# FFN gate and up projections: sixteen tile products per output tile replaced by seven block products

## The chip, the cores and the metric

The kernel runs on one core of a Trainium2 chip. The metric is device time in microseconds (us) for one execution. The engines are named as in the profile: PE (TensorE matmul) and PEld (its weight load), DVE (VectorE), ACT (ScalarE), POOL (GpSimd), and SP, which issues the DMAs.

## What is computed

A decoder trunk of two layers, 512 tokens, model width 1024, FFN width 2816, all in float32. Each layer is an attention mixer and then a SwiGLU FFN, both behind an adaptive norm:

```python
mod = cond @ ada_w[l] + ada_b[l]
sh1, sc1, g1, sh2, sc2, g2 = [m[:, None, :] for m in jnp.split(mod, 6, axis=-1)]
h = _rms_norm(x, norm_mix[l]) * (1.0 + sc1) + sh1
...
x = x + g1 * (y @ w_out[l])
h = _rms_norm(x, norm_ffn[l]) * (1.0 + sc2) + sh2
x = x + g2 * _swiglu(h, ffn_gate[l], ffn_up[l], ffn_down[l])

def _swiglu(h, wg, wu, wd):
    return (jax.nn.silu(h @ wg) * (h @ wu)) @ wd
```

## The kernel before

**Splitting.** Every operand of the large products is held as a pair: `hi`, the value rounded to the PE's fast float32 format (`FR`), and `lo`, what the rounding left. A product is three matmuls, hi with hi, hi with lo and lo with hi, added in PSUM (`mm3`, L437 to L438; the matmul itself is L431, in `mms`). A weight arrives by DMA as a `raw` tile of 128 x 2048 (1 MB) and is split in pieces of 512 columns: ACT copies a piece to `whi` (L457), DVE subtracts to get `wlo` (L473). For some early weights, in the attention, the subtraction of the upper two pieces is on POOL (`prep_to`). Three `raw`, three `whi` and three `wlo` buffers of 2048 columns are there.

**The FFN.** The work is feature-major: an output tile has 128 hidden features on the partitions and the tokens along the columns. There are 22 tiles (`FT`) per layer, in two parts of 11 (`FPARTS`). One unit of weights `wg` holds the gate and up weights of one tile: 8 contraction tiles of 128 for gate, then 8 for up. `ffn_tile` multiplies them with the normalised input `H` (8 tiles, hi and lo):

```python
ps = [self.ps("gu") for _ in range(2)]
for k in range(KT):
    for s in range(2):
        self.mm3(ps[s][:, c], hi[:, s, k], lo[:, s, k], H[k][0][:, c], H[k][1][:, c], k == 0, k == KT - 1)
sg = self.t2("sg")[:, c]
self.act(sg, ps[0][:, c], AF.Silu, after=self.lnexp)
self.tt(sg, ps[1][:, c], sg, OP.mult)
```

and then splits the result into `hid` (ACT copy, DVE subtraction). The first two tiles of a layer are done in token halves of 256 (`HALVES`), since the norm of the second half is not ready when the first is; the other 20 take all 512 tokens at once. After each part, `reduce_out` multiplies the 11 `hid` tiles with the down weights (`wd`) for 8 output tiles and adds them to `x` (L488, `x<-ps,mod,x`).

**Background.** In layer 0's FFN seven modulation vectors of `mod_rest` are computed on DVE beside the rest: each is 16 products of a 128 x 512 piece of `raw<-in_ada` with a column of `cond` (L481 for the first, L488 `t<-raw,cond,t` for those that add), about four such operations for each FFN tile.

**Order.** The builder records operations on virtual tiles; `Sched` puts them in one order with estimated durations (`ve_ns` and others), buffer limits (the groups of `Kern.__init__`) and, for DVE, due times worked out from when PE would want each result. The order of each engine is then fixed in the program. Every engine runs its own list strictly in that order.

Of the kernel before, what the change touches and what calls it, by code (L numbers as in the profile page):

```python
# [20 lines left out]
KT = 8  # L21
# [4 lines left out]
BIG = 1e30  # L26
TOPK = 128
# [50 lines left out]
class View:  # L78
# [32 lines left out]
    def region(self):  # L111
        """bits of the (32-partition quadrant, column block) pairs touched, and elements per partition"""
# [46 lines left out]
class Sched:  # L159
    CROSS, SAME, DMA = 270, 130, 2300  # L160
    # the PE's clock is halved at first and for a while after a long gap
# [54 lines left out]
    def due(self):  # L216
        """priorities from when the PE, kept busy in the present order, would want each result"""
# [151 lines left out]
class Kern:  # L369
    def __init__(self, ctx, tc, io, out):  # L370
        self.ctx, self.tc, self.nc, self.io, self.out = ctx, tc, tc.nc, io, out
        pool = lambda n, b, **k: ctx.enter_context(tc.tile_pool(name=n, bufs=b, **k))
        self.const = pool("const", 1)
        self.s = s = Sched(tc)
        s.group("raw", pool("raw", 3), 3, 0, None)
        s.group("whi", pool("whi", 3), 3, 0, None)
        s.group("wlo", pool("wlo", 3), 3, 0, None)
        n = 61
        s.group("t2", pool("t2", n), n, 8, None, L=12, pT=4, qf=3, q=8, nt=10, hid=26, ada0=20)
        s.group("sm", pool("sm", 80), 80, 16, None)  # L380
        s.group("ps", pool("ps", 8, space=PSUM), 8, 1, None, mm=3, lg=2, tp=2, pv=2, gu=4, st=7)
        self.bg = []

# [38 lines left out]
    def mms(self, jobs, dur=None):  # L422
        """matmuls issued one after the other: (out, stationary, moving, start, stop)"""
# [204 lines left out]
    def mod_first(self, k):  # L628
        """shift and scale of the first norm for the features of k-tile k"""
# [17 lines left out]
    def mod_rest(self, l, v, on_pe):  # L647
        """one of the six modulation vectors"""
        ps = acc = None
        for h in range(4):  # L650
# [3 lines left out]
            for e in range(2):  # L654
# [46 lines left out]
    def norm_stats(self, c, sums=None):  # L701
        """reciprocal root mean square of the tokens c, on every partition"""
# [28 lines left out]
    def proj_f(self, H, i, w, ncol, tag="mm"):  # L731
        """[128 tokens of block i, ncol]; w(k) -> hi, lo of k-tile"""
# [7 lines left out]
    def rstd(self, ss, nh, inv):  # L740
        """[P, nh] of sums of squares -> (ss * inv + eps) ** -0.5"""
# [24 lines left out]
    def q_t(self, ps, qs):  # L766
        """queries of one token block: norm, scale, transpose -> hi, lo [P (two heads), 4, 128 tokens]"""
# [18 lines left out]
    def y_out(self, ps, Y, i, gain=None):  # L786
        """psum [P, 4, 128] -> hi, lo of four k-tiles, tokens of block i"""
# [50 lines left out]
    def idx_scores(self, i, iq):  # L838
# [3 lines left out]
        # Dp is 1e30 where masked, below 512 elsewhere  # L842
# [44 lines left out]
    def pv_t(self, pv, T, src, V):  # L887
        """transposed outputs of eight heads: four on each half of the partitions"""
# [12 lines left out]
    def attn_c(self, i, hg, q, Y):  # L901
        """eight heads of one query block; keys of this block and the one before"""
# [355 lines left out]
```

## Time and profile before

| what | value |
|---|---|
| median of 3 runs | 1208.24 us (1208.17 to 1209.27) |
| profiled execution: span from the first to the last instruction | 1205.3 us |
| median above the span | 2.9 us |
| mean granted TensorE clock | 1.000 |
| PE busy | 1180.9 us, 98% of the span |
| DVE busy | 707.4 us, 59% |
| ACT busy | 487.1 us, 40% |
| POOL busy | 87.9 us, 7% |
| DMA | 151.58 MB, mean 126 GB/s |

The page gives the profiled execution by its span alone, so 2.9 us is what lies around it against the median. Busy time of PE counts matmuls that overlap in the pipeline; how fast matmuls really follow each other is read from the starts in the timeline. The same holds for DVE and ACT: an instruction's duration is somewhat longer than the distance to the next when several stand in a row.

### The profile page before, as it was taken

Reading aid. Unit: us, or ns where it says so; the run is one execution under the profiler, and the core shown is the slowest. Engines: PE = TensorE matmul, PEld = TensorE weight load, DVE = VectorE, ACT = ScalarE, POOL = GpSimd, SP = SyncE. Lnnn points to the kernel's source line nnn. Section 1 sums busy time; section 2 is a strip of 40 time slices with the busy share of each in tenths; the row PEclk is TensorE's granted clock in tenths of the full one; section 3 lists DMA queues with packets and bytes.
Section 4 is the critical chain, followed back from the end, with each engine's and each line's share of the span. In section 5 each row is a group of like instructions: output and inputs, shape, how many; then the busy total and the mean of one; then the engine's idle time right before and its main releaser. Section 6 shows DMA issues by size and latency. Waiting matters only on the chain.

```text
span 1205.3 us, 16639 instructions
## 1 busy us (share of the span) xinstructions
PE 1180.9 (98%) x6424; PEld 956.2 (79%) x6424; DVE 707.4 (59%) x1656; ACT 487.1 (40%) x1194; POOL 87.9 (7%) x224
## 2 busy tenths in 40 slices
PE   6989999999999999999999999999999999999998
PEld 3867667679988888888889876669988888888888
DVE  5599999847875456655443967748633323233321
ACT  5464376755433221232232666755423312223310
POOL 0142332300000000000000120100000000000000
PEclk9999999999999999999999999999999999999999
DMA  9545612202585546655511322011422223322211
GB/s 349 228 140 175 245 41 101 76 31 71 179 299 185 175 155 216 226 189 175 175 59 65 105 71 71 1 71 70 141 105 77 98 88 105 105 105 95 80 53 36
DMA packets 32415, 151.58 MB, mean 126 GB/s; under 512 B 3152, under 2 KB 4304, under 8 KB 21072
## 3 DMA queue, kind: packets, MB, share of 16 engines
q1 hardware_dynamic: 32336, 150.52, 35.6%
q8 instruction: 50, 0.82, 0.3%
q14 instruction: 29, 0.24, 0.1%
HBM read 148.41 MB, written 2.10 MB: 125 GB/s over the span
## 4 chain that ended last, share of the span: by engine, by line
PE 89%; DVE 7%; ACT 2%; issue 1%; POOL 0%; DMA 0%; SPq 0%; DVEq 0%; POOLq 0%; ACTq 0%
PE ps L431 86%; PE ps L442 3%; DVE t L488 2%; ACT t L457 1%; DVE wlo L473 1%; DVE sm L857 1%; DVE t L858 1%; DVE t L473 1%; DVE t L493 1%; DVE t L481 1%; DMA x<-in_x 0%; POOL sm L473 0%; DVE sm L499 0%; ACT whi L457 0%; ACT sm L457 0%
## 5 line engine op out<-in xcount | busy, mean ns | idle before, releaser
L431 PE MATMUL ps<-t,whi 128*128 128x512 f32 (+2 forms) x2864 | 774.7, 358 | 0.9 <-ACT t L457 0.9
L431 PEld LDWEIGHTS ps<-t,whi 128*128 128x128 f32 x2864 | 506.7, 189 | 82.8 <-issue 4.5
L431 PE MATMUL ps<-t,wlo 128*128 128x512 f32 (+2 forms) x1432 | 509.9, 356 | 0.0
L431 PEld LDWEIGHTS ps<-t,wlo 128*128 128x128 f32 x1432 | 270.6, 189 | 38.1
L457 ACT ACTIVATE t<-ps 128x512 f32<-128x512 f32 (+6 forms) x274 | 120.3, 475 | 399.5 <-PE ps L431 372.2
L457 ACT ACTIVATE whi<-raw 128x512 fp32r<-128x512 f32 x364 | 206.8, 621 | 163.3 <-PE ps L431 98.9
L473 DVE TENSOR_TENSOR wlo<-raw,whi 128x512 fp32r<-128x512 f32 x340 | 221.8, 691 | 38.7 <-ACT whi L457 38.3
L473 DVE TENSOR_TENSOR t<-ps,t 128x128 fp32r<-128x128 f32 (+4 forms) x120 | 56.2, 489 | 220.5 <-PE ps L431 202.1
L431 PE MATMUL ps<-whi,t 128*128 128x512 f32 (+1 forms) x512 | 172.9, 394 | 1.1 <-DVE t L488 1.1
L431 PEld LDWEIGHTS ps<-whi,t 128*128 128x128 f32 x512 | 95.0, 189 | 29.5 <-issue 7.8
L488 DVE SCALAR_TENSOR_TENSOR x<-ps,mod,x 128x512 f32<-128x512 f32 (+1 forms) x64 | 39.3, 616 | 115.2 <-PE ps L431 114.7
L431 PE MATMUL ps<-wlo,t 128*128 128x512 f32 (+1 forms) x256 | 96.5, 377 | 0.0
L488 DVE SCALAR_TENSOR_TENSOR t<-raw,cond,t 128x512 f32<-128x512 f32 x112 | 79.1, 761 | 19.5 <-DMA raw<-in_ada 19.5
L431 PE MATMUL ps<-t,t 64*128 64x256 f32 (+5 forms) x592 | 82.8, 347 | 0.2 <-ACT t L457 0.2
L431 PEld LDWEIGHTS ps<-t,t 64*128 64x128 f32 (+2 forms) x592 | 54.3, 181 | 28.4 <-issue 15.1
L457 ACT ACTIVATE t<-t,sm 128x256 f32<-128x256 f32 (+3 forms) x128 | 65.5, 516 | 20.4 <-DVE sm L493 12.6
L442 PE MATMUL ps<-cst,t 128*128 128x128 f32 x388 | 61.8, 279 | 10.0 <-DVE t L473 6.8
L442 PEld LDWEIGHTS ps<-cst,t 128*128 128x128 f32 x388 | 45.0, 140 | 32.6 <-issue 9.9
L481 POOL TENSOR_SCALAR sm<-sm 128x8 f32<-128x8 f32 (+2 forms) x64 | 18.4, 288 | 550.8 <-DVE sm L499 547.4
L473 DVE TENSOR_TENSOR t<-t,t 128x512 fp32r<-128x512 f32 (+3 forms) x85 | 50.2, 593 | 14.1 <-ACT t L457 13.9
L431 PEld LDWEIGHTS ps<-wlo,t 128*128 128x128 f32 x256 | 48.4, 189 | 6.2
L493 DVE CUSTOM_DVE_ANT_0 t<-ps,cst 128x256 f32<-128x256 f32 (+3 forms) x104 | 39.1, 409 | 18.5 <-PE ps L431 18.1
(72 smaller groups left out, 564.6 us busy)
## 6 DMA issues: line engine op xcount, KB each, us to landing
raw<-in_wg SPq DMA_DIRECT2D x44, 1024.0 KB, 4.8
raw<-in_ada SPq DMA_DIRECT2D x40, 1024.0 KB, 5.3
raw<-in_wd SPq DMA_DIRECT2D x20, 1024.0 KB, 4.7
raw<-in_w0c SPq DMA_DIRECT2D x10, 1024.0 KB, 6.1
t<-in_ada SPq DMA_DIRECT2D x32, 256.0 KB, 6.5
raw<-in_wo SPq DMA_DIRECT2D x8, 1024.0 KB, 4.8
raw<-in_w1c SPq DMA_DIRECT2D x6, 1024.0 KB, 4.7
x<-in_x SPq DMA_DIRECT2D x8, 256.0 KB, 5.1
```

The source lines that it names most:

```text
L431: self.nc.tensor.matmul(o.ap(), l.ap(), r.ap(), start=st, stop=sp, skip_group_check=True)
L442: self.s.op("PE", 107, lambda: self.nc.tensor.transpose(out.ap(), src.ap(), self.ident.ap()), [out], [src, self.ident])
L457: self.nc.scalar.activation(out.ap(), src.ap(), func, **kw)
L473: lambda: self.eng(e).tensor_tensor(out.ap(), a.ap(), b.ap(), op=op), [out], [a, b])
L481: self.eng(e).tensor_scalar(out.ap(), a.ap(), val(s1), val(s2), op0=op0, **kw)
L488: lambda: self.nc.vector.scalar_tensor_tensor(out.ap(), a.ap(), val(s), b.ap(), op0=op0, op1=op1),
L493: lambda: self.nc.vector.tensor_tensor_reduce(out.ap(), a.ap(), b.ap(), op0=OP.add, op1=OP.min, scale=scale, scalar=3e38, accum_out=accum. ...
L857: self.s.op("DVE", 65 + 1.05 * n, lambda m8=m8: self.nc.vector.max(m8.ap(), sc.ap()), [m8], [sc])
L858: self.s.op("DVE", 65 + 1.05 * n, lambda m8=m8: self.nc.vector.match_replace(sc.ap(), m8.ap(), sc.ap(), -3e38), [sc], [m8, sc])
```

## The change

For 20 of the 22 FFN tiles of each layer (all but the first two, `DIRECT`), the product of the pair gate and up with the input is written as a 2 x 2 block product: the contraction is cut into halves of 512, the outputs are gate and up, the tokens are cut into halves of 256. Of the eight block products a scheme of Strassen's kind makes seven. It needs sums of weight blocks (four per tile, on POOL, `prep_to`), sums of input blocks (once per layer, `combos`: additions on DVE, four subtractions of 256 columns per contraction tile on POOL, split on ACT and DVE), and sums of the products on the way to gate and up (`ffn_seven`). Each of the seven weight blocks of 512 columns is split into hi and lo as before.

The weight buffers become 26 single tiles of 512 columns (group `w`, in place of 3 + 3 of 2048), the general group goes from 61 to 59 tiles, and gate and up may take six PSUM banks in place of four. The estimate of a POOL operation goes from 2.1 to 2.48 ns per column. The rest of the diff is the same work with the new buffers (`chunk`, `reduce_out`, `ffn_tile`, `even`) and removed comments.

```diff
+NW, NT2 = 26, 59
+DIRECT = 2
...
-        s.group("whi", pool("whi", 3), 3, 0, None)
-        s.group("wlo", pool("wlo", 3), 3, 0, None)
-        n = 61
-        s.group("t2", pool("t2", n), n, 8, None, L=12, pT=4, qf=3, q=8, nt=10, hid=26, ada0=20)
+        s.group("w", pool("w", NW), NW, 6, None)
+        n = NT2
+        s.group("t2", pool("t2", n), n, 8, None, L=12, pT=4, qf=3, q=8, nt=10, hid=26, ada0=20, S=8, T=8)
...
-        s.group("ps", pool("ps", 8, space=PSUM), 8, 1, None, mm=3, lg=2, tp=2, pv=2, gu=4, st=7)
+        s.group("ps", pool("ps", 8, space=PSUM), 8, 1, None, mm=3, lg=2, tp=2, pv=2, gu=6, st=7)
...
         if e == "POOL":
-            return 165 + 2.1 * n
+            return 165 + 2.48 * n
...
-            for a in range(0, w, 512):
-                b = min(a + 512, w)
-                self.copy(hi[:, a:b], raw[:, a:b])
-                self.tt(lo[:, a:b], raw[:, a:b], hi[:, a:b].bitcast(F), OP.subtract, e="POOL" if a >= 1024 and 2 < i < 15 else "DVE")
-            self.ws[i] = (hi, lo)
+            step = 400 if name == "w0s" else 512
+            if name[:2] == "wg" and idx >= DIRECT:
+                X1, X2, Y1, Y2 = (raw[:, a:a + 512] for a in range(0, 2048, 512))
+                S = [self.s.tile("w", "S") for _ in range(4)]
+                for t, x, y, op in ((S[0], Y1, Y2, OP.add), (S[1], S[0], X1, OP.subtract),
+                                    (S[2], X1, Y1, OP.subtract), (S[3], X2, S[1], OP.subtract)):
+                    self.tt(t, x, y, op, e="POOL")
+                src = [X1, S[1], S[0], X2, S[2], S[3], Y2]
+            else:
+                src = [raw[:, a:min(a + step, w)] for a in range(0, w, step)]
+            self.ws[i] = []
+            for j, a in enumerate(src):
+                hi, lo = (self.s.tile("w", "w", dt=FR)[:, :min(step, w - j * step) if len(src) < 7 else 512] for _ in range(2))
+                self.copy(hi, a)
+                self.tt(lo, a, hi.bitcast(F), OP.subtract, e="POOL" if j >= 2 and 2 < i < 15 else "DVE")
+                self.ws[i].append((hi, lo))
...
+    def combos(self, H):
+
+        c1, c2 = HALVES
+        T = []
+        for k in range(4):
+            f = []
+            for j in (k, k + 4):
+                t = self.t2("T")
+                self.tt(t, H[j][0].bitcast(F), H[j][1].bitcast(F), OP.add)
+                f.append(t)
+            p, q = self.t2("T"), self.t2("T")
+            self.tt(p[:, c1], f[0][:, c2], f[0][:, c1], OP.subtract, e="POOL")
+            self.tt(p[:, c2], f[1][:, c2], p[:, c1], OP.subtract, e="POOL")
+            self.tt(q[:, c1], f[1][:, c2], f[0][:, c2], OP.subtract, e="POOL")
+            self.tt(q[:, c2], f[1][:, c1], p[:, c2], OP.subtract, e="POOL")
+            o = []
+            for t in (p, q):
+                hi, lo = self.t2("h", dt=FR), self.t2("h", dt=FR)
+                self.copy(hi, t)
+                self.tt(lo, t, hi.bitcast(F), OP.subtract)
+                o += [(hi[:, c], lo[:, c]) for c in HALVES]
+            T.append(o)
+        return T
+
+    def ffn_seven(self, H, T, w, hid):
+
+        c1, c2 = HALVES
+        a, b, e = (self.ps("gu")[:, c1] for _ in range(3))
+        B11 = [tuple(t[:, c1] for t in H[k]) for k in range(4)]
+        B21 = [tuple(t[:, c1] for t in H[k]) for k in range(4, 8)]
+        B22 = [tuple(t[:, c2] for t in H[k]) for k in range(4, 8)]
+        T1, T2, T3, T4 = ([T[k][j] for k in range(4)] for j in range(4))
+
+        def product(out, j, B, start=False):
+            for k in range(4):
+                wh, wl = (t[:, k * P:(k + 1) * P] for t in w[j])
+                self.mm3(out, wh, wl, B[k][0], B[k][1], start and k == 0, k == 3)
+        pq, u, sg = (self.t2("sg") for _ in range(3))
+        product(a, 0, B11, True)
+        self.copy(pq[:, c1], a)
+        product(b, 1, T2, True)
+        self.tt(b, b, pq[:, c1], OP.add)
+        self.copy(u[:, c1], b)
+        product(e, 2, T1, True)
+        self.copy(pq[:, c2], e)
+        product(a, 3, B21)
+        self.act(sg[:, c1], a, AF.Silu, after=self.lnexp)
+        product(b, 4, T3)
+        self.tt(u[:, c2], b, pq[:, c2], OP.add)
+        product(e, 5, B22)
+        self.tt(sg[:, c2], e, u[:, c1], OP.add)
+        self.act(sg[:, c2], sg[:, c2], AF.Silu)
+        product(b, 6, T4)
+        self.tt(sg[:, c1], b, sg[:, c1], OP.mult)
+        self.tt(sg[:, c2], u[:, c2], sg[:, c2], OP.mult)
+        self.copy(hid[0], sg)
+        self.tt(hid[1], sg, hid[0].bitcast(F), OP.subtract)
+        return sg
...
-                sg = self.ffn_tile(H, f, c, w(f), hid[f - a])
+                if f < DIRECT:
+                    sg = self.ffn_tile(H, f, c, w(f), hid[f - a])
+                else:
+                    T = T or self.combos(H)
+                    sg = self.ffn_seven(H, T, w(f), hid[f - a])
```

What the scheduler makes of it is seen in the engines' own lists. First DVE in the second part of layer 1's FFN, in the middle of the gate and up tiles, before the change (`wlo<-raw,whi` are the weight subtractions; `t<-ps,t` is the product of gate and up, the line with two `t` inputs the subtraction for `hid`):

```order
L473 TENSOR_TENSOR wlo<-raw,whi 128x512 x2
L473 TENSOR_TENSOR t_9999<-ps,t_9999 128x512
L473 TENSOR_TENSOR wlo<-raw,whi 128x512 x2
L473 TENSOR_TENSOR t_10025<-t_9999,t_10018 128x512
L473 TENSOR_TENSOR wlo<-raw,whi 128x512 x2
```

A tile has six DVE instructions of 512 columns there: four weight subtractions, the product and the subtraction. With the change, one tile at the same place (`w<-w` are subtractions on weight sums that POOL made):

```order
L474 TENSOR_TENSOR w<-raw,w 128x512
L474 TENSOR_TENSOR w<-w 128x512 x2
L474 TENSOR_TENSOR ps<-ps,t_13151 128x256
L474 TENSOR_TENSOR w<-raw,w 128x512
L474 TENSOR_TENSOR t_13191<-t_13075,t_13141 128x512
L474 TENSOR_TENSOR w<-w 128x512 x2
L474 TENSOR_TENSOR w<-raw,w 128x512
L474 TENSOR_TENSOR t_13186<-ps,t_13151 128x256
L474 TENSOR_TENSOR t_13217<-ps,t_13186 128x256
L474 TENSOR_TENSOR t_13217<-t_13186,t_13217 128x256
L474 TENSOR_TENSOR t_13217<-ps,t_13217 128x256
```

A tile has thirteen: seven weight subtractions, the `hid` subtraction, and five of 256 columns, one of which puts a sum back into PSUM (`ps<-ps,t`). Nine of the thirteen read two inputs in SBUF, four read PSUM and SBUF.

Then POOL at the start of layer 0's FFN, with the change. Before, POOL has nothing in the FFN: its last instruction on weights is a pair of `wlo<-raw,whi` for `w_out`.

```order
L474 TENSOR_TENSOR w<-raw 128x512
L474 TENSOR_TENSOR w<-w,raw 128x512
L474 TENSOR_TENSOR w<-raw 128x512
L474 TENSOR_TENSOR w<-raw,w 128x512
L474 TENSOR_TENSOR t_3985<-t_3971 128x256
L474 TENSOR_TENSOR t_3985<-t_3995,t_3985 128x256
L474 TENSOR_TENSOR t_4021<-t_3995,t_3971 128x256
```

The four weight sums of the first block-product tile stand ahead of the sixteen input sums of 256 columns, and the four weight sums of the next tile stand among these.

## Rows read from the trace of the kernel before

**Rows 1.** The page: busy time by engine, and the chain's shares.
```profile
PE 1180.9 (98%) x6424; PEld 956.2 (79%) x6424; DVE 707.4 (59%) x1656; ACT 487.1 (40%) x1194; POOL 87.9 (7%) x224
...
PE 89%; DVE 7%; ACT 2%; issue 1%; POOL 0%; DMA 0%; SPq 0%; DVEq 0%; POOLq 0%; ACTq 0%
```

**Rows 2.** Chain in order of time, its last piece: start us, us, what.
```profile
804.87 397.11 PE ps L431 x2048
```

**Rows 3.** Windows, four stretches: us, busy us (count) by engine, clock, DMA.
```profile
312.35:429.07 116.72, 116.72 (x566) 96.22 (x564) 75.03 (x126) 36.92 (x71) 0.00 (x0) 1.00 0.63 218
486.77:613.04 126.27, 126.27 (x574) 102.72 (x574) 64.75 (x106) 38.05 (x70) 0.00 (x0) 1.00 0.50 173
854.54:968.37 113.83, 113.83 (x536) 95.70 (x535) 41.73 (x73) 35.11 (x68) 0.00 (x0) 1.00 0.31 107
1021.48:1147.89 126.41, 126.41 (x559) 104.72 (x558) 43.07 (x71) 36.61 (x69) 0.00 (x0) 1.00 0.29 99
```

**Rows 4.** Timeline of PE in `w_out`, layer 0: start us, us, instruction, count.
```profile
275.85 0.62 PE L431 MATMUL ps<-t,whi 128*128 128x512 f32 x2
...
276.53 0.40 PE L431 MATMUL ps<-t,whi 128*128 128x256 f32 x2
...
287.32 0.40 PE L431 MATMUL ps<-t,whi 128*128 128x256 f32 x2
```

**Rows 5.** Timeline of DVE, FFN of layer 0, instructions in a row.
```profile
477.72 2.50 DVE L473 TENSOR_TENSOR wlo<-raw,whi 128x512 fp32r<-128x512 f32 x4 [1.73 <-ACT whi L457]
480.14 2.73 DVE L488 SCALAR_TENSOR_TENSOR t<-raw,cond,t 128x512 f32<-128x512 f32 x4
...
318.77 1.08 DVE L473 TENSOR_TENSOR t<-ps,t 128x256 f32<-128x256 f32 x3
```

**Rows 6.** Lines by form: count, busy us, mean ns of one, idle before.
```profile
L473 DVE TENSOR_TENSOR wlo<-raw,whi 128x512 fp32r<-128x512 f32 x339 | 221.5, 692 | 38.7 <-ACT whi L457 38.3
L473 POOL TENSOR_TENSOR wlo<-raw,whi 128x512 fp32r<-128x512 f32 x24 | 34.1, 1435 | 77.4 <-ACT whi L457 77.3
L488 DVE SCALAR_TENSOR_TENSOR t<-raw,cond,t 128x512 f32<-128x512 f32 x112 | 79.1, 761 | 19.5 <-DMA raw<-in_ada 19.5
L473 DVE TENSOR_TENSOR t<-ps,t 128x256 f32<-128x256 f32 x8 | 3.1, 418 | 3.9 <-ACT t L457 3.9
L473 POOL TENSOR_TENSOR sm<-sm 128x8 f32<-128x8 f32 x60 | 16.0, 267 | 23.2 <-ACT sm L457 20.2
```

**Rows 7.** Timeline of POOL and DVE, attention of layer 0, 63 to 70 us.
```profile
63.70 1.29 POOL L473 TENSOR_TENSOR wlo<-raw,whi 128x512 fp32r<-128x512 f32 x1 [0.38 <-ACT whi L457]
63.75 0.48 DVE L473 TENSOR_TENSOR t<-ps,t 128x128 fp32r<-128x128 f32 x2
64.15 1.39 DVE L473 TENSOR_TENSOR wlo<-raw,whi 128x512 fp32r<-128x512 f32 x1
...
66.90 1.63 DVE L473 TENSOR_TENSOR wlo<-raw,whi 128x512 fp32r<-128x512 f32 x1
67.95 1.74 POOL L473 TENSOR_TENSOR wlo<-raw,whi 128x512 fp32r<-128x512 f32 x1
68.46 1.78 DVE L473 TENSOR_TENSOR wlo<-raw,whi 128x512 fp32r<-128x512 f32 x1
```

**Rows 8.** The same two engines, attention of layer 0, at 100 and 174 us.
```profile
100.66 2.55 POOL L473 TENSOR_TENSOR wlo<-raw,whi 128x512 fp32r<-128x512 f32 x2 [3.86 <-ACT whi L457]
...
101.45 1.15 DVE L857 MAX8 sm<-t 128x8 f32<-128x512 f32 x2
...
174.54 1.54 POOL L473 TENSOR_TENSOR wlo<-raw,whi 128x512 fp32r<-128x512 f32 x1 [0.58 <-ACT whi L457]
...
174.19 2.44 DVE L488 SCALAR_TENSOR_TENSOR t<-raw,cond,t 128x512 f32<-128x512 f32 x2
...
177.38 1.46 DVE L488 SCALAR_TENSOR_TENSOR t<-raw,cond,t 128x512 f32<-128x512 f32 x1
```

**Rows 9.** Timeline of ACT, start of layer 1's FFN: the last half-tile silu.
```profile
862.58 0.38 ACT L457 ACTIVATE t<-ps 128x256 f32<-128x256 f32 x1 [2.02 <-PE ps L431]
```

More of the change, by code (lines that the diff above doesn't have):

```diff
@@ L482, in ts, with stt @@
         self.s.op(e, self.ve_ns(e, out.region()[1], a.base.group != "ps", len(ptr)), fn, [out], [a] + ptr)
-    def stt(self, out, a, s, b, op0, op1):
+    def stt(self, out, a, s, b, op0, op1, e="DVE"):
         ptr = [s] if isinstance(s, View) else []
         val = lambda v: v.ap() if isinstance(v, View) else v
-        self.s.op("DVE", self.ve_ns("DVE", out.region()[1], False, len(ptr)),
-                  lambda: self.nc.vector.scalar_tensor_tensor(out.ap(), a.ap(), val(s), b.ap(), op0=op0, op1=op1),
+        self.s.op(e, self.ve_ns(e, out.region()[1], False, len(ptr)),
+                  lambda: self.eng(e).scalar_tensor_tensor(out.ap(), a.ap(), val(s), b.ap(), op0=op0, op1=op1),
                   [out], [a, b] + ptr)
@@ L550, in prep_to @@
             w = self.units[i][2]
+            name, idx, _ = self.units[i]
             raw = self.raws.pop(i)
-            hi = self.s.tile("whi", "whi", (P, 2048), FR)
-            lo = self.s.tile("wlo", "wlo", (P, 2048), FR)
-            for a in range(0, w, 512):
-                b = min(a + 512, w)
-                self.copy(hi[:, a:b], raw[:, a:b])
-                self.tt(lo[:, a:b], raw[:, a:b], hi[:, a:b].bitcast(F), OP.subtract, e="POOL" if a >= 1024 and 2 < i < 15 else "DVE")
-            self.ws[i] = (hi, lo)
+            step = 400 if name == "w0s" else 512
[14 more added lines that the diff above has]
+                self.ws[i].append((hi, lo))
             self.prepped += 1
@@ L568, in chunk @@
     def chunk(self):
-        ua, ub = self.unit(), self.unit(2)
-        a, b = ([t.rearrange("p (k c) -> p k c", k=4) for t in u] for u in (ua, ub))
-        return lambda k: (a[0][:, k], a[1][:, k]) if k < 4 else (b[0][:, k - 4], b[1][:, k - 4])
+        ts = self.unit() + self.unit(2)
+        return lambda k: ts[k]
     def setup(self):
@@ L645, in mod_first, with mod_rest @@
         self.stt(self.G[0][0][:, k:k + 1], self.mod[0][:, 1, k:k + 1], 1.0, self.ng[:, 0, 0, k:k + 1], OP.add, OP.mult)
-    def mod_rest(self, l, v, on_pe):
+    def mod_rest(self, l, v, on_pe, e_="DVE"):
         ps = acc = None
@@ L951, in even @@
         self.score, self.iw, self.bv = {}, {}, {}
-        hi, lo = self.unit()
-        hi, lo = (t[:, :1600].rearrange("p (k c) -> p k c", k=8) for t in (hi, lo))
-        small = [self.proj_f(H, i, lambda k: (hi[:, k], lo[:, k]), 200, "st") for i in range(NB)]
+        ws = self.unit()
+        w0s = lambda k: tuple(t[:, (k % 2) * 200:(k % 2) * 200 + 200] for t in ws[k // 2])
+        small = [self.proj_f(H, i, w0s, 200, "st") for i in range(NB)]
         w = self.chunk()
@@ L1077, in block @@
             while len(blocks) <= j:
-                hi, lo = self.unit()
+                u = self.unit()
                 w = self.units[self.cursor - 1][2]
-                blocks.extend((hi[:, a:a + P], lo[:, a:a + P]) for a in range(0, w, P))
+                blocks.extend(tuple(t[:, a % 512:a % 512 + P] for t in u[a // 512]) for a in range(0, w, P))
             return blocks[j]
@@ L1104, in ffn_tile @@
             for s in range(2):
-                self.mm3(ps[s][:, c], hi[:, s, k], lo[:, s, k], H[k][0][:, c], H[k][1][:, c], k == 0, k == KT - 1)
+                wh, wl = (t[:, (k % 4) * P:(k % 4) * P + P] for t in w[2 * s + k // 4])
+                self.mm3(ps[s][:, c], wh, wl, H[k][0][:, c], H[k][1][:, c], k == 0, k == KT - 1)
         sg = self.t2("sg")[:, c]
@@ L1113, in ffn @@
     def ffn(self, l, H, last):
+        T = None
         for pi, (a, b) in enumerate(FPARTS):
@@ L1119, in w @@
                 if f not in W:
-                    W[f] = [t.rearrange("p (s k c) -> p s k c", s=2, k=8) for t in self.unit()]
+                    W[f] = self.unit()
                 return W[f]
@@ L1123, in ffn @@
             if pi == 0:
-                jobs = [(a + e, c) for c in HALVES for e in range(2)]
+                jobs = [(a + e, c) for c in HALVES for e in range(DIRECT)]
             jobs += [(f, ALL) for f in range(a + len(jobs) // 2, b)]
             for f, c in jobs:
-                sg = self.ffn_tile(H, f, c, w(f), hid[f - a])
+                if f < DIRECT:
[3 more added lines that the diff above has]
+                    sg = self.ffn_seven(H, T, w(f), hid[f - a])
                 self.lnexp = []
```

5 lines of the change are left out of this document (2 added, 3 removed).

## The prediction

> **What bounds the kernel now.** I read the page first: PE is busy for 98% of the span and holds 89% of the chain that ended last [rows 1]. The chain's last piece is 397.11 us of matmuls without a break, all of layer 1's FFN [rows 2]. So there only PE's own work counts, or whatever makes PE wait anew. The change touches four stretches, which the windows show [rows 3]: from the end of the norm to the first update of `x` (layer 0: A0, 116.7 us; layer 1: A1, 113.8 us), and from the last update of part 1 to the first of part 2 (B0, 126.3 us; B1, 126.4 us). PE is busy through all four, POOL does nothing, DVE works 75.0, 64.8, 41.7 and 43.1 us. Everything else, some 720 us, I take as unchanged: the same work with other buffers. Its order moves in places; the chain has 9% on DVE and ACT [rows 1], about 108 us, and a twentieth of that, 5 us either way, goes into the range (a choice).
>
> **PE: what the change takes away.** Matmuls of 512 columns start 0.68 us apart in threes (275.85 to 276.53), so 0.227 us each; of 256 columns 30 threes take 10.79 us (276.53 to 287.32), so 0.120 us each [rows 4]. A tile had 2 x 8 x 3 = 48 of the first kind, 10.88 us. It gets 7 x 4 x 3 = 84 of the second, 10.07 us. The eighth of the products that goes is mostly eaten by the dearer short matmul: 0.8 us is left per tile. That is 7.2 us in A0 and A1 (nine tiles), 8.8 us in B0 and B1 (eleven), 32 us in all.
>
> The Trainium skill (TensorE: Matmul & The Clock Gate, section Back-to-back issue gap) gives columns / 2.4 + 2.5 ns for matmuls in a row, so 216 and 109 ns; by that a tile would save 1.2 us, and the 40 tiles 15 us more than by the rows. The rows are of this kernel with its weight loads and decide.
>
> **DVE: what it adds.** In a row, 512-column subtractions come every 0.603 us ((2.50 - 0.69) / 3), background steps every 0.657 us ((2.73 - 0.76) / 3), 256-column operations every 0.33 us ((1.08 - 0.42) / 2) [rows 5, 6]. A tile had 6 x 0.603 = 3.6 us and gets 8 x 0.603 + 5 x 0.33 = 6.5 us. The input sums add 16 x 0.603 = 9.6 us per layer. On the windows of [rows 3] this gives A0 75.0 + 9 x 2.9 + 9.6 = 111, B0 97, A1 77, B1 75 us. Counting the changed DVE list between the same marks gives 105, 95, 76 and 74 (in A0 a few background steps now stand outside); I use these. All fit under PE's time. ACT gains three copies and some halves, about 3 us per tile; with 35 to 38 us in stretches of 114 to 126 us [rows 3] it stays below PE. No DMA is added, and SP issues in the same order.
>
> **POOL and DVE together.** POOL gets four 512-column operations per tile, some 1.3 us each when alone [rows 7], 5.2 us per tile of 10: it is not the bound itself. But it stood idle in the FFN, and the trace shows what it does to DVE. At 64 us DVE subtractions that read two SBUF inputs take 1.39, 1.63 and 1.78 us beside POOL's [rows 7], against 0.69 alone [rows 6]; POOL's fourth takes 1.74 us in place of 1.29. They take turns: DVE's end at 68.53 and 70.24, a period of 1.71 us for one of each. At 174 us two background steps take 2.44 us beside one POOL operation, against 0.76 + 0.657 in a row; one takes 1.46 [rows 8]. DVE operations that read PSUM, or one input, are not held up (0.48 us for two at 63.75, `MAX8` at 101.45) [rows 7, 8].
>
> So I charge DVE a wait d for each POOL operation of 512 columns. The hits cost 0.70, 0.94, 1.09, 1.03 and 0.70 us, mean 0.89. Bounds: 0, as beside `MAX8`, and 1.09. In the changed list 9 of 13 operations per tile read two SBUF inputs, and in layer 0 the background steps come on top, so nearly each POOL operation should hit: I take 0.89. POOL's 16 input sums of 256 columns cost (1435 + 267) / 2 = 0.85 us each [rows 6] and hold DVE about half as long. A0 has 32 + 8, the other stretches 40 such units (those of the first tile come earlier): 40 x 0.89 = 36 us more for DVE.
>
> The Trainium skill (SBUF — State Buffer, section Who interferes with whom) says that with two SBUF inputs on DVE against a reading GpSimd instruction the second to start fully blocks until the first is done. Taken at its word, every POOL operation would cost DVE its whole length, which is the third rival below; by the rows, where a pair overlaps by about 0.2 us and some waits are partial, it is less.
>
> **The start of each FFN.** The input sums need the whole norm. In layer 1 it ends at 854.5 [rows 3] and the half tiles at about 862.6 [rows 9]. POOL then has 16 x 0.85 + 4 x 1.3 = 19 us in a row, plus about 2 us for the split behind it: T complete at about 875 to 880. PE has, without T, two products of each of two tiles, 48 x 0.12 = 5.8 us, and half of T's products, 2.9 us: until 871. I take 8 us of waiting per layer (0 to 12).
>
> **The shared PSUM bank.** In `ffn_seven` the product that ends in `b` needs DVE's reading of `b` one product earlier: 12 matmuls, 1.44 us of cover. One subtraction in the way and the 0.42 us reading take 1.11 us, but 2.2 us when POOL is in the way (1.78 + 0.42) [rows 6, 7]. That is 0 to 0.8 us per tile; I take 0.4 for the 20 tiles of layer 1, 8 us. In layer 0 DVE's time counts it already.
>
> **The sum.** A0: DVE 105 + 36 = 141 against 116.7, +24. B0: 95 + 36 = 131 against 126.3, +5. A1: the larger of DVE 76 + 36 = 112 and PE 113.8 - 7.2 + 8 = 114.6, +1. B1: the larger of 74 + 36 = 110 and PE 117.6, -9. The bank +8. Together +29 us on the span of 1205.3, or 1237 us on the median of 1208.2, which lies 2.9 us above the span.
>
> **Rivals.** *DVE's waits are absorbed; faster.* POOL's operations could fall where DVE waits for PE, or beside its PSUM reads. With d = 0 all four stretches go at PE's pace: +1, -9, +1, -9, no bank waits: 1192 us, or 1176 us without waits at the start. For it: DVE has 40 us free in A1 and 52 us in B1; beside `MAX8` nothing was lost [rows 8]. Against it: in A0 and B0 hardly anything is free. It decides at d of about 0.5, where A0 costs 8, B1 and B0 give 9 each, and start and bank take 9 back.
>
> *DVE's waits are longer; slower still.* With d = 1.09 A0 is 149 us (+32), B0 139 (+12), A1 120 (+6), B1 -9; with 0.8 us at the bank, 16: +57, 1265 us. For it: DVE and POOL run in fixed orders, so one late step delays all behind it. Against it: PSUM reads, a third of the list, go through.
>
> *Each POOL operation holds DVE for its full length.* 40 x 1.29 = 52 us a stretch [rows 7]: A0 157 us (+40), B0 147 (+20), A1 128 (+14), B1 126 (-1), bank 8: +81, 1289 us. Against it: none of the five hits cost more than 1.09 us. The rule that fits is the one cited above from the Trainium skill (SBUF — State Buffer).
>
> *The weights come too late; slower.* A tile needs 14 hi and lo slots and four sums of the 26 slots, so PE's lead is under two tiles where it was three. If the chain of three dependent POOL sums (3 x 1.74 = 5.2 us [rows 7]), copy and subtraction were exposed by 2 us per tile, 40 tiles would give 80 us less the 32: 1256 us, or 1285 us on top of the waits forecast. Against it: POOL is done in about 7 of 10 us per tile even when it takes turns. The change does what it says in any case: POOL's list holds the sums (its rows stand with the change).
>
> **How the numbers follow.** The forecast (1215 to 1260) gets 0.54, the first rival 0.23, the second 0.12, the third 0.04, the fourth 0.04; 0.03 is left for an end within 0.2%, which is about what a measurement of this kernel can tell from no change. So faster 0.23, same 0.03, slower 0.74. The range goes from 1192, the first rival's own time, to 1275, 10 us above the second's: that leaves out the corner without any wait, the third rival and part of the fourth.
>
> **What would show it.** Matmuls of 256 columns at 0.12 us apart in rows of 12; DVE subtractions in the FFN at a mean well above 0.69 us (about 1.0) while those on PSUM stay at 0.42; POOL sums at 1.4 to 1.8 us; DVE above 90% busy in A0 and B0, with PE waiting for DVE there; a wait of PE of about 8 us before the first block-product tile; B1 shorter than before. It is wrong if DVE's subtractions stay at 0.69 us, if the four stretches come out at 117, 118, 115 and 118 us, or if PE waits for ACT or POOL rather than DVE.

## The result, and the profile after

The changed kernel takes **1267.21 us** (median, 1265.76 to 1270.39) against 1208.2: ratio 1.0496, 95% interval 1.0477 to 1.0515, so 59 us slower. 1237 was forecast, with a range of 1192 to 1275. The profiled execution, the longest of the four, has a span of 1268.6 us: 63 us above the span before, where the medians differ by 59. Of all executions below, one of `e3_combos_dve` (1316.5 us) was in a slower state of the chip, at a clock of 0.84, and is left out.

The page of the changed kernel: busy time, PE's granted clock in 40 slices (tenths), and the chain's shares.

```profile
PE 1184.5 (93%) x7864; PEld 1023.4 (81%) x7864; DVE 981.6 (77%) x1968; ACT 617.3 (49%) x1490; POOL 366.7 (29%) x416
...
PEclk9999999999889999988899999999979999999999
...
PE 67%; DVE 26%; issue 3%; ACT 2%; POOL 1%; DMA 0%; SPq 0%; DVEq 0%; POOLq 0%
```

Against [rows 1] DVE has 274 us more work and takes 26% of the chain in place of 7%; PE is idle for 84 us of the span, and its clock is not full everywhere. To place the loss I cut both kernels at their updates of `x` (in the timeline). A0 and A1 begin here at the last update of `w_out`, so that they hold the norm too (15 us more than in [rows 3]); B0 and B1 run from the last update of part 1 to the first of part 2. Windows of the kernel before (us, busy us and count of PE, PEld, DVE, ACT, POOL, clock, DMA; A0, B0, A1, B1):

```profile
297.29:429.07 131.78, 131.78 (x690) 111.23 (x688) 89.92 (x160) 47.20 (x93) 0.00 (x0) 1.00 0.58 201
486.02:613.04 127.02, 127.02 (x578) 103.35 (x577) 65.50 (x108) 38.05 (x70) 0.00 (x0) 1.00 0.50 174
839.49:968.37 128.88, 128.88 (x660) 110.69 (x659) 56.49 (x106) 44.66 (x88) 0.00 (x0) 1.00 0.30 102
1020.73:1147.89 127.16, 127.16 (x562) 105.33 (x561) 43.82 (x72) 37.36 (x70) 0.00 (x0) 1.00 0.29 101
```

The same four of the changed kernel:

```profile
303.04:462.13 159.09, 134.84 (x993) 127.93 (x993) 157.65 (x235) 75.08 (x161) 69.34 (x48) 0.94 0.42 149
517.51:664.33 146.82, 131.02 (x970) 125.57 (x970) 130.11 (x188) 71.13 (x149) 54.92 (x36) 0.93 0.46 160
893.18:1036.41 143.23, 126.70 (x969) 123.04 (x968) 127.75 (x188) 77.42 (x162) 68.29 (x48) 0.95 0.25 85
1088.77:1211.23 122.46, 119.73 (x958) 117.37 (x957) 103.07 (x149) 69.55 (x147) 55.07 (x36) 1.00 0.31 108
```

| stretch | forecast | measured |
|---|---|---|
| A0 | +24 | +27.3 |
| B0 | +5 | +19.8 |
| A1 | +1, bank +4 | +14.3 |
| B1 | -9, bank +4 | -4.7 |
| `w_out` with the first half norm, layers 0 and 1 | 0 | +5.5, +1.8 |
| all else | 0 | -0.7 |
| sum | +29 | +63.3, the difference of the spans |

A0 and B1 are close; B0 and A1 carry most of the miss. In A0 DVE works 99% of the time. In B0 it works 130 us, as forecast (131), but the stretch takes 147: PE idles 15.8 us, DVE 16.7.

Lines by form, changed kernel (count, busy us, mean ns of one, idle before):

```profile
L474 DVE TENSOR_TENSOR w<-raw,w 128x512 fp32r<-128x512 f32 x296 | 246.9, 846 | 43.8 <-ACT w L458 43.0
L474 DVE TENSOR_TENSOR w<-w 128x512 fp32r<-128x512 f32 x160 | 142.0, 911 | 10.8 <-ACT w L458 6.6 <-PE ps L432 4.2
L489 DVE SCALAR_TENSOR_TENSOR t<-raw,cond,t 128x512 f32<-128x512 f32 x112 | 92.4, 870 | 7.3 <-DMA raw<-in_ada 7.3
L474 DVE TENSOR_TENSOR t<-ps,t 128x256 f32<-128x256 f32 x128 | 51.8, 415 | 16.4 <-PE ps L432 16.1 <-ACT w L458 0.2
L482 DVE TENSOR_SCALAR t<-raw,cond 128x512 f32<-128x512 f32 x16 | 12.3, 779 | 0.0
L474 POOL TENSOR_TENSOR w<-raw 128x512 f32<-128x512 f32 x80 | 125.8, 1573 | 359.6 <-PE ps L432 202.6 <-DMA raw<-in_wg 77.3 <-ACT w L458 36.7
L474 POOL TENSOR_TENSOR t<-t,t 128x256 f32<-128x256 f32 x24 | 25.0, 1065 | 1.7 <-DVE t L474 1.4
L458 ACT ACTIVATE w<-w 128x512 fp32r<-128x512 f32 x160 | 98.2, 623 | 31.9 <-PE ps L432 15.6 <-DVE w L474 11.9 <-POOL w L474 4.3
```

Subtractions went from 692 to 846 and 911 ns, background additions from 761 to 870 [rows 6], while operations on PSUM stay at 415. How that reaches PE shows in the timeline of the changed kernel, one tile of B0 (start, us; POOL, DVE, PE):

```profile
539.99 1.71 POOL L474 TENSOR_TENSOR w<-raw 128x512 f32<-128x512 f32 x1 [2.54 <-PE ps L432]
...
545.05 1.47 POOL L474 TENSOR_TENSOR w<-raw,w 128x512 f32<-128x512 f32 x1
...
542.17 0.42 DVE L474 TENSOR_TENSOR ps<-ps,t 128x256 f32<-128x256 f32 x1
542.50 1.43 DVE L474 TENSOR_TENSOR w<-w 128x512 fp32r<-128x512 f32 x1
543.86 1.52 DVE L482 TENSOR_SCALAR t<-raw,cond 128x512 f32<-128x512 f32 x1
545.30 1.77 DVE L474 TENSOR_TENSOR w<-w 128x512 fp32r<-128x512 f32 x1
547.00 0.47 DVE L482 TENSOR_SCALAR t<-raw,cond 128x512 f32<-128x512 f32 x1
...
548.66 0.41 DVE L474 TENSOR_TENSOR t<-ps,t 128x256 f32<-128x256 f32 x1
...
543.06 3.49 PE L432 MATMUL ps<-t,w 128*128 128x256 f32 x27 [0.28 <-ACT t L458]
549.13 11.46 PE L432 MATMUL ps<-t,w 128*128 128x256 f32 x81 [2.57 <-DVE t L474]
```

Four POOL sums in a row (539.99 to 546.5) stretch DVE's instructions to 1.4 to 1.8 us; the reading of the shared bank stands behind them (548.66), and PE waits 2.57 us for it. Then the clock falls. Windows of that place:

```profile
545.50:549.50 4.00, 1.43 (x12) 1.22 (x12) 4.00 (x6) 0.63 (x1) 1.02 (x1) 1.00 0.14 16
549.50:553.50 4.00, 4.00 (x24) 4.00 (x23) 3.12 (x7) 1.78 (x4) 0.00 (x0) 0.57 0.87 351
```

After a pause in which PE worked 1.43 of 4 us the granted clock is mostly at its lower level, 1.2 of 2.4 GHz, over the next 4 us, and PE starts 24 matmuls where 4.0 / 0.12 = 33 would fit.

### The profile page after: what moved, and what is told of

Same layout as the page of the kernel before. It is cut to its first block, busy times and chain, and to the rows that moved or that the text cites. A ratio compares the mean times of both kernels' runs of the same rounds, so it can differ in the third digit from the quotient of the medians.

```text
span 1268.6 us, 20661 instructions
## 1 busy us (share of the span) xinstructions
PE 1184.5 (93%) x7864; PEld 1023.4 (81%) x7864; DVE 981.6 (77%) x1968; ACT 617.3 (49%) x1490; POOL 366.7 (29%) x416
## 4 chain that ended last, share of the span: by engine, by line
PE 67%; DVE 26%; issue 3%; ACT 2%; POOL 1%; DMA 0%; SPq 0%; DVEq 0%; POOLq 0%
PE ps L432 63%; DVE w L474 12%; DVE t L474 6%; DVE t L489 6%; PE ps L443 4%; ACT t L458 1%; DVE t L482 1%; ACT w L458 1%; DVE t L868 1%; DVE sm L867 1%; DVE t L494 1%; DMA x<-in_x 0%; DVE ps L474 0%; POOL t L474 0%; DVE x L489 0%
## 5 line engine op out<-in xcount | busy, mean ns | idle before, releaser
L432 PE MATMUL ps<-t,w 128*128 128x256 f32 (+2 forms) x5736 | 845.6, 309 | 59.1 <-DVE t L474 40.3
L432 PEld LDWEIGHTS ps<-t,w 128*128 128x128 f32 x5736 | 781.1, 196 | 114.3 <-DVE t L474 45.8
L474 DVE TENSOR_TENSOR w<-raw,w 128x512 fp32r<-128x512 f32 (+1 forms) x300 | 248.9, 843 | 43.8 <-ACT w L458 43.0
L458 ACT ACTIVATE w<-raw 128x512 fp32r<-128x512 f32 (+1 forms) x324 | 195.9, 625 | 145.8 <-PE ps L432 104.2
L458 ACT ACTIVATE t<-ps 128x256 f32<-128x256 f32 (+6 forms) x394 | 155.9, 426 | 184.9 <-PE ps L432 126.3
L474 POOL TENSOR_TENSOR w<-raw 128x512 f32<-128x512 f32 x80 | 125.8, 1573 | 359.6 <-PE ps L432 202.6
L432 PE MATMUL ps<-w,t 128*128 128x512 f32 (+1 forms) x768 | 190.6, 391 | 1.6 <-DVE t L489 1.4
L432 PEld LDWEIGHTS ps<-w,t 128*128 128x128 f32 x768 | 133.2, 190 | 35.3 <-issue 6.7
L474 DVE TENSOR_TENSOR w<-w 128x512 fp32r<-128x512 f32 x160 | 142.0, 911 | 10.8 <-ACT w L458 6.6
L474 DVE TENSOR_TENSOR t<-t,t 128x256 f32<-128x256 f32 (+3 forms) x157 | 115.1, 746 | 20.9 <-ACT t L458 20.3
```

The source lines that it names most:

```text
L432: self.nc.tensor.matmul(o.ap(), l.ap(), r.ap(), start=st, stop=sp, skip_group_check=True)
L458: self.nc.scalar.activation(out.ap(), src.ap(), func, **kw)
L474: lambda: self.eng(e).tensor_tensor(out.ap(), a.ap(), b.ap(), op=op), [out], [a, b])
```

## The experiments

All times are medians beside runs of the kernel before (1207.1 to 1207.6) on the same chip. In `e1` to `e5`, `e7`, `e11`, `e13` and `e14` the planner sees the same instructions with the same estimates as in the changed kernel, so the order is its order; only what is issued at a place differs.

**Which part costs: the sums on POOL.** `e1_no_sums`:

```diff
-                    self.tt(t, x, y, op, e="POOL")
+                    self.s.op("POOL", self.ve_ns("POOL", 512, False), lambda: None, [t], [x, y])
...
-                self.copy(hi, a)
+                d = self.smt if len(src) == 7 and j in (1, 2, 4, 5) else a
```

> Every engine's list is that of the changed kernel; only the four weight sums per tile on POOL are not issued, and the copies and subtractions of those four blocks read a constant tile instead (so seven-tile outputs are not the reference's). Turn-taking (POOL's operations hold DVE's two-input ones): DVE's weight subtractions go back from 846 to about 700 ns, A0 and B0 come back to near PE's pace but for the start wait; 1205 to 1225 us. DVE's own work is the cause (rival): DVE's list is as long as before, so 1250 us or more. Late weights (26 slots, chain of sums): the chain is gone too, 1195 to 1215 us, so this run does not tell that one from turn-taking.

1195.0 us, ratio 0.9894 (0.9874 to 0.9914): 10 us below the band for turn-taking, and at the lower edge of the one for late weights, which this run cannot tell apart. Subtractions are back at 698 ns. Windows of this run, the same four stretches:

```profile
297.14:434.09 136.95, 128.89 (x1010) 124.75 (x1009) 129.64 (x233) 75.77 (x163) 17.54 (x16) 0.98 0.49 174
487.70:608.72 121.02, 121.02 (x985) 117.81 (x985) 99.50 (x188) 71.35 (x150) 0.00 (x0) 1.00 0.56 195
834.35:963.52 129.17, 124.45 (x984) 122.04 (x983) 101.58 (x187) 77.18 (x162) 18.64 (x16) 0.99 0.28 94
1015.88:1134.26 118.38, 118.38 (x958) 117.05 (x957) 79.66 (x148) 70.01 (x146) 0.00 (x0) 1.00 0.33 112
```

PE never waits in B0 and B1; B1 is 8.8 us shorter than before, the eleven tiles times 0.8 us of the forecast. The sums cost 72 us in all. DVE's longer list alone is not the cause: it is still there. `e4_sums_memset` issues `memset(t)` on POOL in place of each sum:

> The same lists, but each weight sum on POOL is a memset of the same 512 columns: POOL writes SBUF and reads nothing (so the sums hold a constant and the seven-tile outputs are not the reference's). If only POOL's reading (two inputs) holds DVE, as the rows with two readers suggest: 1205 to 1225 us, like the run without sums. If any POOL access does, in proportion to its length: DVE's weight subtractions stay above 780 ns and the time at 1225 to 1260 us.

1194.4 us, ratio 0.9890 (0.9871 to 0.9908): like the run without sums, as expected for reading alone, though again below the band. Its lines by form, DVE and POOL:

```profile
L474 DVE TENSOR_TENSOR w<-w 128x512 fp32r<-128x512 f32 x160 | 108.8, 703 | 13.0 <-ACT w L458 8.9 <-PE ps L432 3.8
L561 POOL MEMSET w<- 128x512 f32 x160 | 83.5, 531 | 474.2 <-PE ps L432 426.0 <-DVE w L474 42.0 <-DVE t L489 3.9
```

A POOL operation that only writes SBUF holds nobody here: DVE's subtractions take 703 ns beside 160 memsets and 700 without them. As the 26 slots are as many here, they are not what costs: the fourth rival falls, but for a lateness from the sums' own length. Against that speaks the trace of the changed kernel: ACT's 160 copies of the sums waited for POOL for 4.3 us in all (the last line by form in the section on the result). `e2_sums_dve` issues the four sums on DVE, `self.nc.vector.tensor_tensor(...)` at POOL's places:

> The same lists, but the four weight sums per tile are issued on DVE at the places where the planner had put them for POOL. Turn-taking: DVE gets 4 x 0.603 = 2.4 us more per tile, 22 to 27 us per stretch, but loses the waits (36 us or more per stretch by the prediction): A0 105 + 22 + start, B0 95 + 27 = 122, A1 and B1 at PE's pace; 1205 to 1235 us. DVE's own work is the cause: slower than the changed kernel, 1285 us or more. Late weights: the chain of sums now stands in DVE's queue behind other work, 1267 us or more.

1221.4 us, ratio 1.0109 (1.0088 to 1.0131). 160 x 0.603 = 96 us more work on DVE costs less than half of what the same sums cost on POOL. B0 took 124.5 us with DVE busy for 118.9, B1 118.4 with 100.4.

**The start.** `e3_combos_dve` moves only the sixteen subtractions of `combos` to DVE, `e5_all_dve` these and the weight sums.

> The same lists, but the sixteen input sums of 256 columns per layer are issued on DVE (0.33 us each, 5.3 us per layer) in place of POOL; the weight sums stay on POOL. If the input sums on POOL, and what they do to DVE's additions beside them, make the wait at the start of the block products and the drop of the granted clock there, A0 loses 8 to 12 us and A1 6 to 10: 1245 to 1255 us. If the start is late for the weights' sake, no change: 1265 to 1270 us.

1261.2 us, ratio 1.0446 (1.0417 to 1.0474): 6.0 us less than the changed kernel, 2.8 in A0 and 3.6 in A1 by the profile, between the two bands; beside the weight sums, moving them helps little.

> The same lists as the changed kernel, with both the weight sums and the input sums issued on DVE at the places the planner had given them on POOL; POOL then does nothing in the FFN but what it did before. The run with the weight sums alone on DVE gave 1221.4 us, with 19.0 and 9.2 us of PE's waits in A0 and A1. If POOL's input sums make the waits at the start, those fall by 4 to 8 us per layer: 1208 to 1215 us. If the start waits for DVE's own additions and subtractions after the norm, and POOL has no part in it: 1219 to 1224 us.

1212.0 us, ratio 1.0033 (1.0021 to 1.0046): 9.4 us less than `e2_sums_dve`, as expected. PE's waits are 14.2 us in A0 and 5.9 in A1 against 19.0 and 9.2. With no POOL in it at all, the change is slower than before by 0.3%.

**The parts costed at nothing, and DVE's load.** `e6_buffers_only` computes every tile the old way (`idx >= 22`, `f < 22`) with the new buffers:

> The changed kernel's buffers, caps and estimates, but every FFN tile is computed as before the change (no sums, no block products). The prediction costs this part at nothing: 1205 to 1211 us. If the single weight tiles or the fewer slots cost something by themselves: 1214 us or more.

1207.5 us, ratio 0.9998 (0.9988 to 1.0007): right. `e7_bg_out` does not issue the additions of `mod_rest` (`lambda: None`):

> The changed kernel without the background additions (15 of every 16 steps of the modulation vectors on DVE are not issued, so those vectors are not the reference's); everything else in the same lists. It takes some 45 steps out of DVE's list in A0 and 34 in B0, 0.66 to 0.87 us each. If PE's pauses come from a late DVE queue (turn-taking plus its load), A0 becomes like A1 (159 to about 140 us) and B0 like B1 (147 to 121 to 127): 1222 to 1232 us. If POOL's holds alone decide, whatever DVE has to do: A0 falls by what DVE saves, but B0 stays above 140: 1245 us or more.

1237.7 us, ratio 1.0251 (1.0236 to 1.0267): near the first theory, not in its band. A0 fell to 143.2 us, like A1, but B0 to 132.6 only, with DVE busy for 105.8 us and PE still waiting 9.0. So DVE's load counts, and it need not be full for POOL's holds to reach PE.

**Clock, bank, order.** `e11_filler` keeps PE busy in B0's pauses:

```diff
                if j == 6 and k == 0 and fill:
...
+                        for i in range(12):
+                            mm(o2, w5[0], B22[3][0], True, True)
```

> The changed kernel's lists with twelve extra matmuls of 256 columns (1.44 us at the full clock, into a half bank that nobody reads) ahead of the seventh product, where PE waits for DVE, in the eleven tiles of B0 alone: 15.8 us of work, most of it inside pauses of 1.9 to 2.9 us. If PE's pauses are what brings the granted clock down, the clock of B0 stays at 1.00 (a deficit of under 3 us in place of 10.3) and B0 takes 139 to 146 us: 1258 to 1267 us. If the clock falls for another reason, the deficit stays at 8 us or more and B0 at 149 or more: 1270 to 1278 us.

1268.9 us, ratio 1.0506 (1.0489 to 1.0524), between the bands. B0's window in this run:

```profile
518.66:666.16 147.50, 139.28 (x1104) 134.04 (x1103) 129.49 (x187) 71.34 (x149) 55.62 (x36) 0.99 0.46 161
```

From its timeline of PE (L1164 holds the filler and the matmuls behind it) a pause, the last pause of B0 and the two fillers after it; then the last pause of the changed kernel:

```profile
550.01 1.60 PE L1164 MATMUL ps<-t,w 128*128 128x256 f32 x12
552.22 0.62 PE L1164 MATMUL ps<-t,w 128*128 128x256 f32 x3 [0.61 <-DVE t L474]
...
633.91 0.63 PE L1164 MATMUL ps<-t,w 128*128 128x256 f32 x3 [0.72 <-DVE t L474]
...
646.61 1.96 PE L1164 MATMUL ps<-t,w 128*128 128x256 f32 x15
...
654.53 1.96 PE L1164 MATMUL ps<-t,w 128*128 128x256 f32 x15
...
634.96 22.16 PE L432 MATMUL ps<-t,w 128*128 128x256 f32 x177 [1.11 <-DVE t L474]
```

The clock stays up (0.99 against 0.93), so the pauses are what lowers it. Yet B0 takes 147.5 us, as long as without. At the pauses PE still waits for DVE behind the filler: DVE's queue sets the pace, and the slower clock mostly fills time that PE would have waited. It is not quite free: the last pause ends 115.3 us into B0 (633.91 less 518.66) against 117.5 in the changed kernel (634.96 less 517.51), 2.2 us sooner, but the two fillers behind it, where nothing is waited for, cost 2.9 us.

`e9_fourth_bank` gives the seventh product a bank of its own (`product(d, 6, T4, True)`, then `self.tt(d, d, pq[:, c1], OP.add)`):

> The changed kernel with a fourth PSUM bank per tile: the seventh product goes into a bank of its own, so that PE no longer waits for DVE's reading of the shared bank one product earlier; for it DVE adds one 256-column sum and ACT one copy per tile (order planned anew). If the handoff of the shared bank is where PE's pauses come from, PE's waits in B0 (15.8 us) and behind the start in A1 go to a third and the granted clock stays up there: B0 147 to about 134, A1 143 to about 136, B1 122.5 to about 119.5, A0 (DVE full) 3 us longer; 1240 to 1252 us. If DVE's late queue only makes PE wait at the next place that needs it: 1260 to 1272 us.

1261.5 us, ratio 1.0448 (1.0431 to 1.0464). In the changed kernel all of PE's waits for DVE in B0 stand ahead of this product (in `e11_filler` the seven fall on L1164). PE's waits in B0, changed kernel and this run (total, times, longest):

```profile
PE ps L432 <- DVE t L474: 15.0, 7, 2.9
...
PE ps L432 <- ACT t L458: 11.7, 7, 3.1
PE ps L432 <- DVE t L489: 4.3, 2, 3.3
```

The waits for DVE fell from 15.0 to 4.3 us, but 11.7 us for ACT's copies, which wait for DVE themselves, came in their place: 16.0 us of idle PE as before. `e10_planner_est` gives the weight subtractions of block-product tiles 65 + 1.6 x 512 = 884 ns in the plan:

> The changed kernel, but the planner is told 884 ns for a weight subtraction of a block-product tile on DVE in place of 597, near the 846 to 911 ns measured beside POOL; work and engines are the same, only the order moves. If part of the loss is that the planned order puts subtractions and background steps ahead of the readings that PE waits for: 1245 to 1260 us. If the loss lies in the holds whatever the order: 1262 to 1272 us.

1266.4 us, ratio 1.0490 (1.0471 to 1.0508): no change. This other order loses as much; more were not tried.

**Burst or number.** `e13_spread` adds `for _ in range(2): self.nc.gpsimd.memset(t.ap(), 0.0)` ahead of the later three sums of a tile:

> The changed kernel's lists; ahead of the second, third and fourth weight sum of a tile POOL also writes the sum's own buffer twice with a memset (0.53 us each, which holds nobody), so that the four sums of a tile stand about 1 us apart instead of back to back. The holds are as many and as long. If the loss in B0 and A1 comes from the burst (some 6.5 us in which DVE goes at half its pace while PE runs on to the next reading it needs), PE's waits in B0 fall from 15.8 to under 9 us and B0 from 147 to 138 or less: 1240 to 1257 us. If the sum of the holds counts, however spread: 1262 to 1272 us. If the later sums make the weights late: 1275 us or more.

1265.1 us, ratio 1.0473 (1.0459 to 1.0487). B0 went to 142.1 and A1 to 140.6, A0 to 162.7. In B0 PE's waits for DVE fell from 15.0 to 7.7 us, but those for ACT rose from 0.8 to 6.1, and ACT itself waited 10.7 us for sums that now end later, against 0.9. So spreading gains 5 us in B0; what the burst alone costs stays open, as part of its gain may go to the later sums. `e14_half` leaves `S[0]` and `S[2]` on POOL and puts the other two on DVE:

> The changed kernel's lists with two of the four weight sums per tile on POOL and two on DVE. All on POOL is 1267 us, all on DVE 1221. If the loss goes with the number of holds: halfway, 1238 to 1250 us. If only a burst of holds longer than what PE's lead covers costs time: 1222 to 1234 us.

1242.3 us, ratio 1.0283 (1.0269 to 1.0297), 2 us from the middle of 1221.4 and 1267.2: the loss goes with the number of sums on POOL.

**A faster version.** From all this: block products where DVE has room, no sums on POOL, input sums ahead of need. `e8_part2_dve`:

```diff
+SEVEN = {0: 11, 1: 11}
...
-                    self.tt(t, x, y, op, e="POOL")
+                    self.tt(t, x, y, op, e="DVE")
...
+                self.run_bg(3 if pi == 0 else 2)
+            if pi == 0 and SEVEN[l] < 22:
+                T = self.combos(H)
```

> Block products only in the second part of each layer's FFN (11 of 22 tiles), input sums made on DVE under the reduce ahead of it, weight sums on DVE, more of the background steps in part 1 (three per tile in place of two); first parts as before the change, order planned anew. From the run with weight sums on DVE, B1 took 118.4 us against 127.2 and B0 124.5 against 127.0 with 24 more background steps than here. If PE's pace is all that is left in B0 and B1: 1208 - 2 x 8.8 = 1190 us, up to 1195. If DVE still binds in B0 (its list there is 198 instructions), B0 gives 3 us: 1196 to 1199. If the input sums and the extra background steps disturb the stretches ahead: 1203 us or more.

1189.0 us, ratio 0.9847 (0.9832 to 0.9862). `e12_more_tiles` has `SEVEN = {0: 11, 1: 5}`:

> The faster version (block products in the second parts, all sums on DVE), with block products also for the last six tiles of layer 1's first part, and the input sums made beside the five tiles ahead of them. PE gains 6 x 0.8 = 4.8 us if DVE, whose list in A1 then fills some 120 of 124 us, never makes PE wait: 1183 to 1186 us against 1189.0. If it does: 1188 us or more.

1185.2 us, ratio **0.9816** (0.9802 to 0.9831), the lowest median of all: 22 us less than before. Its windows, A0, B0, A1, B1:

```profile
298.45:433.58 135.13, 135.13 (x709) 113.38 (x708) 115.02 (x206) 51.37 (x97) 0.00 (x0) 1.00 0.66 235
487.00:605.33 118.33, 118.33 (x959) 116.44 (x959) 106.32 (x200) 71.84 (x148) 0.00 (x0) 1.00 0.41 148
830.96:958.28 127.32, 126.69 (x885) 118.87 (x884) 105.43 (x206) 68.62 (x139) 0.00 (x0) 1.00 0.27 96
1008.60:1126.98 118.38, 118.38 (x958) 117.06 (x957) 100.33 (x185) 70.99 (x147) 0.00 (x0) 1.00 0.32 112
```

PE hardly waits, and both second parts go at 118.4 us. `e15_more_tiles2` has `SEVEN = {0: 9, 1: 3}`:

> The faster version with more block-product tiles in the first parts: layer 0 from the tenth tile, layer 1 from the fourth (1185.2 us with none and with six). 4 more tiles x 0.8 = 3.2 us if DVE keeps up: 1181 to 1184 us. If its list, some 120 us in both first parts, makes PE wait: 1185 us or more.

1186.8 us, ratio 0.9829 (0.9814 to 0.9844): PE waits 1.6 and 1.5 us in A0 and A1, so DVE's room is used up. The intervals of these two runs overlap: four more tiles gain nothing clear.

## Why the prediction was right in sign and too small

**PE's saving: right.** 8.8 us less in B1 wherever PE does not wait; the first rival's 1192 us, PE's pace with waits at the start alone, is what the kernel without sums gives (1195.0).

**DVE and POOL: right mechanism, size a little high.** DVE's busy time is 981.6 us with the sums and 862.0 without: 119.6 us over 160 sums, 0.75 us each, where I took 0.89. That DVE's total in B0 came out as forecast is in part luck: without the sums its list took 99.5 us there, not 95, and the 36 sums of that window added 30.6 us, not 36. That POOL must read is shown by the memsets. The Trainium skill (SBUF — State Buffer, section Who interferes with whom) says that two SBUF inputs on DVE contend with a GpSimd instruction that reads, not with one that only writes: the runs agree. The full block, which the same page states for such a pair (section SBUF: two separate sides, not the one that the prediction names) and which the third rival used, would be an estimated 1.29 us for each sum that meets DVE; the traces show 0.75 on average over all sums.

**The sum: this step failed.** I wrote "B0: 95 + 36 = 131 against 126.3, +5" and "A1: the larger of DVE 76 + 36 = 112 and PE ... 114.6, +1", and of the bank "in layer 0 DVE's time counts it already". Each stretch was taken as the longer of two sums of work, so that DVE's free time could absorb holds anywhere. DVE's 130 us in B0 was right, the 147 of the stretch was not, and the bank, at nothing in layer 0, is where PE waited 15.0 us in B0. Of 119.6 us that the sums take from DVE, 72 reach the end, 60%; my sum let 45 of 144 through (the forecast less the first rival), 31%. My reading is that PE meets DVE several times in each tile, with a lead of less than two tiles, and a hold ahead of such a point is not made up later: PE pauses there, and DVE in turn waits for the products that come late (both idle some 16 us in B0). That the loss follows the sums on POOL is shown (all four on DVE: 1221, two: 1242, none: 1267; not issued: 1195). How exactly they turn into B0's 16 us is not settled: neither the bank, the one other order, nor the clock alone explains it; the burst's share is open, and deeper buffers were not tried.

**The start: too small.** I took 8 us of PE's waits. The window of the start of the block products in A1, changed kernel:

```profile
917.00:945.00 28.00, 16.87 (x100) 15.86 (x100) 26.36 (x29) 11.22 (x27) 22.19 (x19) 0.76 0.21 76
```

The timeline of PE and POOL there:

```profile
923.76 6.84 PE L432 MATMUL ps<-t,w 128*128 128x256 f32 x36 [5.71 <-DVE w L474]
938.83 11.37 PE L432 MATMUL ps<-t,w 128*128 128x256 f32 x79 [4.09 <-DVE t L474]
...
908.08 3.87 POOL L474 TENSOR_TENSOR t<-t 128x256 f32<-128x256 f32 x1 [17.81 <-DVE t L474]
928.97 4.36 POOL L474 TENSOR_TENSOR t<-t,t 128x256 f32<-128x256 f32 x4
```

PE idles 11.1 of these 28 us and goes at a mean clock of 0.76. The input sums took 1.07 us and more each beside DVE, not 0.85, and POOL's row ends at 933 after 25 us, not 19. With the input sums still on POOL but no weight sums, PE idles 4.7 us in all of A1 (`e1_no_sums`) against 16.5 here, so the weight sums make most of this.

**Left out.** The clock (a mean of 0.976, nowhere in the sum) accompanies the pauses. PE's busy time in the four stretches is 512.3 us against 492.7 without the sums; in B0, where it is 10 us more, about 2 reached the end (`e11_filler`), and elsewhere this was not tried. The first tile's weight sums already run beside the norm of the half tiles: four `t<-x,G,t` at 296.01 take 4.39 us, which is part of the +5.5 in `w_out`. The second rival came close (1265) for the wrong reason: it assumed holds of 1.09 us. The third rival's +20 in B0 and +14 in A1 are what was measured, by chance: it needs DVE busy for 147 and 128 us there, and DVE worked 130 and about 113 (127.8 less some 15 for the norm).

## What to carry to other kernels

Work given to an idle POOL is not free when it reads SBUF: here each 512-column sum took 0.75 us from DVE, and the same sums on DVE itself cost 46 us less. The longer of two engines' work sums is a lower bound for a stretch; where the engines hand over several times per tile, price a share of the delay even when the total leaves room. And place an arithmetic saving where its helper work has a cover: 28 of the 40 block-product tiles, with their sums on DVE, gained 22 us once they stood where DVE had room.

## What was not expected of the hardware

- A DVE `TENSOR_SCALAR` with one SBUF input, which I took as not held, went from a mean of 480 ns before to 779 ns with POOL's sums, and back to 508 without them; the one at 543.86, beside a sum, took 1.52 us, the one at 547.00, beside none, 0.47. The Trainium skill (SBUF — State Buffer, section Who interferes with whom) names `tensor_scalar` among the operations that can take the shared ports; the trace agrees, and I had read the rows for other one-input operations as if they held for it.
- POOL does not always get its turn after one DVE instruction. Timeline of the changed kernel, DVE, beside POOL's operation of 3.87 us at 908.08 above:

```profile
908.26 3.09 DVE L474 TENSOR_TENSOR t<-t,t 128x512 f32<-128x512 f32 x5
```

Five additions in a row went by at 0.6 us each, at their usual pace, while POOL's one subtraction, 0.74 us at best (928.28), took 3.87.

- The clock fell behind pauses such as the 2.57 us at 549.13; in B1, whose longest pause is 1.1 us, it stayed at 1.00.
